# A first modulation in plain float32 on four column quarters, a fixed order of its loads, and sums over partitions that end in a transpose

## Chip, cores and metric

One core of a Trainium2 chip (trn2) runs the whole program once. The metric is the device time of one execution in microseconds; the median of several executions counts.

## What is computed

Two blocks of two layers each, on 256 tokens of width 1024. The change lies almost wholly in the first block. Cut to what matters:

```
xl, xc = x, ctx                                  # 256 tokens each, width 1024
for l in range(2):
    mod  = silu(c)     @ w_mod[l] + b_mod[l]     # 1024 -> 6 * 1024
    modc = silu(c_ctx) @ w_mod[l] + b_mod[l]
    sh1, sc1, gt1, sh2, sc2, gt2 = split(mod, 6) # same for modc
    h = rms_norm(xl, g_pre_mix[l]) * (1 + sc1) + sh1        # and hc from xc
    y, yc = token_mixer(h, hc, ..., w_in[l], ...)
    xl = xl + gt1 * rms_norm(y, g_post_mix[l])
    h = rms_norm(xl, g_pre_ffn[l]) * (1 + sc2) + sh2
    xl = xl + gt2 * rms_norm(swiglu(h, w_ffn_in[l], w_ffn_out[l]), g_post_ffn[l])
    # layer 0 does the same for xc
```

The second block has two more layers with attention and an FFN of the same size; it needs no modulation, but its norms use the same sums.

## The kernel before, in words

Activations lie feature-major: 128 features on the partitions, tokens along the columns (512 columns while both streams run, 256 later). A float32 product is made of three matmuls in the `float32r` type (`mm3`, L164 to L166): high part times high part, high times low, low times high. Weights come in loads of 1 MB (`raw`, L124, two buffers, issued by SP); each is cut into two pieces, and for each piece ACT makes the high part (`whi`, L154) and DVE or POOL the low part (`wlo`, L155). Four pieces (`RING`) can stand ready. A planner (`emit`) calls each piece's `prep` as soon as the ring has room, in the order in which the steps of the program use the pieces. A scheduling layer then puts each engine's instructions in an order of its own; only what is pinned (`pin`) keeps the order of the program.

The program's beginning is what the change touches most. `setup` loads `c`, `c_ctx` (SP) and `x`, `ctx` (ACT) and makes silu(c) as `st1`, 128 columns wide per feature block and zero but for four columns: two streams, each as a high and a low part. `mod(l, g)` (L433 on) makes 512 of the 6144 columns of the modulation. It loads eight tiles of 128 x 512 from `w_mod`, splits every one (ACT L257, DVE L258), and does two matmuls of 512 columns per tile (L447, L448). `mod_flush` copies the 32 rows out on ACT (L502), transposes them on DVE (L503), adds high and low parts in four pieces (L507) and adds the bias (L510). For layer 0 the four groups 2, 3, 0, 1 are done so, 32 tiles in all: these are `sc1` and `sh1`. Between the first two groups stands `x_in`: squares of the input rows on ACT (L1096), 32 transposes on PE (L1106), 1/rms on DVE. Then `pre0` broadcasts 1/rms over the partitions (L316) and makes the eight pairs of high and low parts of `h` (`norm_mod`: DVE L558, ACT L560, DVE L561); the mixer's first matmul with `w_in` needs the first pair.

All other groups of the modulation are made on DVE while PE works at something else (`mod_v`): a loaded half (`mraw`, L458, two buffers) is multiplied by silu(c), one scalar per partition, and added up (L478), and the sum over the 128 partitions is left to PE. `flush` does that with four matmuls per stream that have 128 columns of the sums as the stationary operand and one column of ones as the moving one (L484). The norms take their sums over the features in the same way: `y_rms` after the mixer and the FFN (L611, L612; for three quantities when the residual's norm is made at once), `col_rms` elsewhere (L307).

```
nc.tensor.matmul(ps[:, 4 * i + t:4 * i + t + 1], accs[g][i][:, 128 * t:128 * t + 128],
                 self.ones[:, 0:1], start=True, stop=True)
```

Of the kernel before, what the change touches and what calls it, by code (L numbers as in the profile page):

```python
# [14 lines left out]
D = 1024  # L15
# [30 lines left out]
class Kern:  # L46
# [64 lines left out]
    def pieces(self, loads, na, nb, cuts, perm=False):  # L111
        box = {}
        out = []
        for i, (a0, a1, b0, b1) in enumerate(cuts):
# [3 lines left out]
            def prep(p=p, i=i, a0=a0, a1=a1, b0=b0, b1=b1):  # L118
                nc = self.nc
                if i == 0:  # L120
                    raw = self.static("raw", 2048, RAWS)
                    box["raw"] = raw[:, : na * nb].rearrange("p (a b) -> p a b", a=na)
                    for view, src in loads:
                        nc.sync.dma_start(view(box["raw"]), src)  # L124
                src = box["raw"][:, a0:a1, b0:b1]
# [17 lines left out]
                if perm:  # L143
                    assert a0 == 0 and a1 == na and hb == 128
                    for q in range(2):
                        for h2 in range(2):
                            s_ = src[:, :, 64 * h2:64 * h2 + 64].rearrange(
                                "p a (b q i) -> p a q b i", b=2, q=2, i=16)[:, :, q]
                            o = [x[:, :, 64 * h2:64 * h2 + 64].rearrange(
                                "p a (q b i) -> p a q b i", b=2, q=2, i=16)[:, :, q] for x in (p.hi, p.lo)]  # L150
                            nc.scalar.activation(o[0], s_, AF.Copy)
                            eng.tensor_tensor(o[1], s_, o[0], op=ALU.subtract)
                else:
                    nc.scalar.activation(p.hi, src, AF.Copy)  # L154
                    eng.tensor_tensor(p.lo, src, p.hi, op=ALU.subtract)  # L155

# [11 lines left out]
    def lin(self, st, W, c0, ncols, rhs, N, evac, perm=False, K=8, tok=None, order=None):  # L168
# [5 lines left out]
        for c in range(0, ncols, wide):  # L174
# [4 lines left out]
            for i, p in enumerate(ps_):  # L179
                for j in range(0, cuts[i][3] - cuts[i][2], 128):  # L180
                    def run(t0, t1, p=p, j=j):
                        ps = self.lin_ps()
                        r = rhs()
                        for i, k in enumerate(order or range(K)):
                            rk = [v[:, t0:t1] for v in r[k]]
                            self.mm3(ps[:, t0:t1], (p.hi[:, k, j:j + 128], p.lo[:, k, j:j + 128]), rk,
                                     i == 0, i == K - 1)
                        return ps
# [9 lines left out]
                    st.append(("x", cost, f, (p,), [lambda t=t, run=run, m=m: evac(m, run(*t), t)  # L198
                                                    for t in ((0, N // 2), (N // 2, N))]))

# [100 lines left out]
    def col_rms(self, key, nt, dim):  # L301

        nc = self.nc
        acc = self.v.pop(key)
        ps = self.tr_ps()
        for t in range(nt):
            nc.tensor.matmul(ps[:, t:t + 1], acc[:, 128 * t:128 * t + 128], self.ones[:, 0:1], start=True, stop=True)  # L307
        v = self.small([128, nt])
        nc.vector.tensor_scalar(v, ps[:, :nt], 1.0 / dim, EPS, op0=ALU.mult, op1=ALU.add)
        return self.rsqrt(v, nt)  # L310
# [32 lines left out]
    def setup(self):  # L343
# [8 lines left out]
        nc.vector.memset(self.ones, 1.0)  # L352
        self.twos = self.const([128, 1], "twos")
        nc.vector.memset(self.twos, 2.0)
# [12 lines left out]
        nc.vector.tensor_tensor(cc, cc, th, op=ALU.mult)  # L367
        self.st1 = self.const([128, 8, 128], "st1", F32R)
        nc.vector.memset(self.st1.bitcast(F32), 0.0)
        v = cc.rearrange("p (s k) -> p k s", s=2)  # L370
        nc.vector.tensor_copy(self.st1[:, :, 0:2], v)
        nc.vector.tensor_tensor(self.st1[:, :, 2:4], v, self.st1[:, :, 0:2], op=ALU.subtract)
        self.cc = cc
# [58 lines left out]

    def mod(self, l, g):  # L433

        nc = self.nc
        raw = []
        for k in range(8):
            w = self.slot()
            nc.sync.dma_start(w, self.a["w_mod"][l, 128 * k:128 * k + 128, 512 * g:512 * g + 512])
            raw.append(w)  # L440

        def f():
            ps = self.lin_ps()
            for k in range(8):
# [11 lines left out]
    def mraw(self, l, g, h):  # L456
        w = self.wp.tile([128, 2, 512], F32, name=self.nm("mraw"), tag="mraw", bufs=MRAWS)
        self.nc.sync.dma_start(w, self.a["w_mod"][l, 256 * h:256 * h + 256, 512 * g:512 * g + 512].rearrange(  # L458
            "(k p) c -> p k c", p=128))
        return w  # L460

    def mod_v(self, st, l, groups, streams):
# [17 lines left out]
        def flush(g):  # L480
            ps = self.tr_ps()
            for i in range(streams):
                for t in range(4):
                    nc.tensor.matmul(ps[:, 4 * i + t:4 * i + t + 1], accs[g][i][:, 128 * t:128 * t + 128],  # L484
                                     self.ones[:, 0:1], start=True, stop=True)
            del accs[g]
            b = self.par["b_mod", l][:, 4 * g:4 * g + 4]
            for i in range(streams):
                nc.vector.tensor_tensor(self.mc[l][:, 4 * g:4 * g + 4, i], ps[:, 4 * i:4 * i + 4], b, op=ALU.add)

# [5 lines left out]
        st.append(("x", 0.05, lambda: flush(groups[-1])))  # L496

    def mod_flush(self, l, g, ps):
        nc = self.nc
        rw = self.slot()  # L500
        tw = self.slot()
        nc.scalar.activation(rw[0:32, :], ps[0:32, :], AF.Copy)  # L502
        nc.vector.transpose(tw[0:32, :], rw[0:32, :])  # L503
        v = tw[0:32, :].rearrange("p (t q r) -> p t q r", t=4, q=4)
        mc = self.mc[l]
        for q in range(4):
            nc.vector.tensor_tensor(mc[32 * q:32 * q + 32, 4 * g:4 * g + 4, :], v[:, :, q, 0:2], v[:, :, q, 2:4],  # L507
                                    op=ALU.add)
        b = self.par["b_mod", l][:, 4 * g:4 * g + 4]
        nc.vector.tensor_tensor(mc[:, 4 * g:4 * g + 4, :], mc[:, 4 * g:4 * g + 4, :],  # L510
                                b[:, :, None].to_broadcast([128, 4, 2]), op=ALU.add)

# [57 lines left out]
    def y_add(self, m, ps, tok, full):  # L570
# [26 lines left out]
        if full:  # L597
            put(1, lambda o: nc.vector.tensor_tensor(o[:, c], z[:, c], x[:, c], op=ALU.mult))
            put(2, lambda o: nc.scalar.activation(o[:, c], z[:, c], AF.Square))

    def y_rms(self, t0, full):

        nc, V = self.nc, self.v
        n = 3 if full else 1
        ps = self.tr_ps()
        for i in range(n):
            for t in range(2):
                c = slice(t0 + 128 * t, t0 + 128 * t + 128)
                o = ps[:, 2 * i + t:2 * i + t + 1]
                w = self.ones[:, 0:1] if i != 1 else self.twos  # L610
                nc.tensor.matmul(o, V["acc", i][:, c], w, start=True, stop=False)  # L611
                nc.tensor.matmul(o, V["last", i][:, c], w, start=False, stop=True)  # L612
        v = self.small([128, 2])
        nc.vector.tensor_scalar(v, ps[:, 0:2], 1.0 / D, EPS, op0=ALU.mult, op1=ALU.add)
        if full:
            S = self.small([128, 4])
            nc.vector.tensor_copy(S, ps[:, 2:6])
        r = self.rsqrt(v, 2)
        out = self.bcast(r, 2)
        V["rb"] = out  # L620
        if full:
# [4 lines left out]
            for t in range(2):  # L626
                c = slice(t, t + 1)
                nc.vector.scalar_tensor_tensor(b[:, c], S[:, 2 + t:3 + t], r[:, c], S[:, c], op0=ALU.mult, op1=ALU.add)
            for t in range(2):
# [455 lines left out]
    def block1(self):  # L1085
# [27 lines left out]
        def pre(l, N, t0, s_scale, s_shift, gain):  # L1113
# [4 lines left out]
            return lambda i, rb, t1: self.norm_mod(i, t0, t1, rb, V["A"], self.sec(l, s_shift))  # L1118

        def pre0():  # L1120
            f = pre(0, 512, 0, 1, 0, "g_pre_mix")
            rb = self.bcast(V["r0"], 4)
            for i in range(8):
                f(i, rb, 512)

        def join(l, N, t0, s_scale, s_shift, gain, hot):
# [9 lines left out]
        for l in range(2):  # L1136
            N = 512 if l == 0 else 256
            if l == 0:
                fs = [self.mod(0, g) for g in (2, 3, 0, 1)]
                st.append(X(fs[0]))  # L1140
                st.append(X(x_in))
                st += [X(f) for f in fs[1:]]
                st.append(H(pre0))
# [18 lines left out]
            P_ = lambda p: st.append(X(lambda: setattr(self, "phase", p), 0))  # L1162
            P_(2 * l)
            st += mix
            P_(2 * l + 1)
# [649 lines left out]
def emit(steps, bufs):  # L1815
# [11 lines left out]
    for i, s in enumerate(steps):  # L1827
        if len(s) > 3:
            while nxt < len(order):
                p = order[nxt]  # L1830
                j = p.at - bufs[p.ring]
                if j >= 0 and rings[p.ring][j].end >= i:
                    break
                p.prep()
                nxt += 1
# [85 lines left out]
```

## Time and profile before

| | |
|---|---|
| three runs | 2300.19, 2303.47, 2305.83 us (median 2303.47) |
| the profiled execution | 2300.08 us, span of the profile 2297.9 us |
| PE busy | 2172.5 us, 95% of the span |
| DVE, ACT, POOL busy | 1622.3, 1083.9, 508.1 us |
| mean granted TensorE clock | 0.969 of 2.4 GHz |

The span is read from the first instruction to the last; 2.2 us of the execution lie outside it. A busy PE is not a PE at its peak, since matmuls overlap: their ends are modelled, and a matmul's price is read from one start to the next. A float32 matmul (not `float32r`) stands in the trace as two records. Column counts in the rows are partitions x elements, the stationary operand with a `*`.

### The profile page before, as it was taken

How to read it: one execution, taken by the hardware profiler on the slowest of the kernel's cores; microseconds unless marked ns; L12 is line 12 of the kernel's file. 1: busy time of each engine (PE TensorE's matmuls, PEld its weight loads, DVE VectorE, ACT ScalarE, POOL GpSimd, SP SyncE). 2: the span in 40 equal slices, each digit the busy share in tenths (PEclk: the TensorE clock that was granted, in tenths of full speed). 3: DMA queues.
4: the chain of work that ended last, by engine and by line, in shares of the span. 5: the costliest groups of instructions: out<-in, count | busy, mean ns of one | idle time of the engine just before them, and what ended most of it. 6: DMA issues, size and time to landing. Idle time of an engine off the chain costs nothing.

```text
span 2297.9 us, 37350 instructions
## 1 busy us (share of the span) xinstructions
PE 2172.5 (95%) x14512; PEld 1970.2 (86%) x14512; DVE 1622.3 (71%) x3259; ACT 1083.9 (47%) x2098; POOL 508.1 (22%) x513
## 2 busy tenths in 40 slices
PE   4999999999989999998999899999978999999998
PEld 3777777788888888888888899899976999988998
DVE  5577777858778845567978877765685766676665
ACT  5355565332432222244556555554446544466443
POOL 2354443321230011032333311100243100110000
PEclk8999999999989999998999999999997999999999
DMA  8321112335515656444322455465441555543553
GB/s 277 79 90 56 56 56 74 114 132 180 165 38 159 187 179 199 155 155 128 119 74 86 136 175 178 137 203 183 152 114 53 166 183 181 194 154 105 183 180 120
DMA packets 296626, 319.18 MB, mean 139 GB/s; under 512 B 20545, under 2 KB 264353, under 8 KB 296449
## 3 DMA queue, kind: packets, MB, share of 16 engines
q1 hardware_dynamic: 293072, 311.27, 42.0%
q0 software_dynamic: 2224, 3.43, 0.6%
q8 instruction: 114, 1.87, 0.3%
q10 hardware_dynamic: 1152, 2.10, 0.3%
q14 instruction: 64, 0.52, 0.1%
HBM read 315.72 MB, written 1.05 MB: 138 GB/s over the span
## 4 chain that ended last, share of the span: by engine, by line
PE 71%; DVE 16%; ACT 5%; issue 4%; DMA 2%; POOL 1%; ACTq 0%; DVEq 0%; POOLq 0%; SPq 0%
PE p L164 20%; PE p L165 20%; PE p L166 20%; DVE wlo L155 3%; DVE t L796 1%; PE p L743 1%; DVE t L478 1%; PE p L247 1%; PE p L249 1%; PE tr L883 1%; PE p L248 1%; DVE b L855 1%; PE tr L484 1%; DVE t L258 1%; ACT whi L154 1%
## 5 line engine op out<-in xcount | busy, mean ns | idle before, releaser
L164 PE MATMUL p<-t,whi 128*128 128x256 f32 (+1 forms) x3724 | 1177.1, 320 | 12.6 <-ACT t L560 6.3
L165 PE MATMUL p<-t,whi 128*128 128x256 f32 (+1 forms) x3724 | 1178.3, 317 | 6.3 <-DVE t L659 3.1
L166 PE MATMUL p<-t,wlo 128*128 128x256 f32 (+1 forms) x3724 | 1176.6, 317 | 2.9 <-DVE wlo L155 1.6
L164 PEld LDWEIGHTS p<-t,whi 128*128 128x128 f32 x3724 | 715.8, 194 | 63.8 <-ACT t L560 7.9
L165 PEld LDWEIGHTS p<-t,whi 128*128 128x128 f32 x3724 | 719.8, 193 | 50.4 <-DVE t L659 4.5
L166 PEld LDWEIGHTS p<-t,wlo 128*128 128x128 f32 x3724 | 718.7, 193 | 47.9 <-DVE wlo L155 3.2
L154 ACT ACTIVATE whi<-raw 128x1024 fp32r<-128x1024 f32 (+4 forms) x487 | 491.8, 1020 | 522.9 <-PE p L165 341.5
L155 DVE TENSOR_TENSOR wlo<-raw,whi 128x1024 fp32r<-128x1024 f32 (+4 forms) x443 | 546.1, 1234 | 184.8 <-ACT whi L154 86.5
L155 POOL TENSOR_TENSOR wlo<-raw,whi 128x1024 fp32r<-128x1024 f32 (+2 forms) x44 | 104.2, 2368 | 505.1 <-ACT whi L154 462.7
L478 DVE SCALAR_TENSOR_TENSOR t<-mraw,big,t 128x512 f32<-128x512 f32 x224 | 166.6, 782 | 24.7 <-DMA mraw<-in_w_mod_dram 23.4
L794 POOL TENSOR_TENSOR t<-t,t 128x512 f32<-128x512 f32 (+1 forms) x120 | 137.6, 1147 | 190.0 <-ACT t L793 187.4
L260 ACT ACTIVATE t<-t 128x256 fp32r<-128x256 f32 (+1 forms) x115 | 54.4, 473 | 160.6 <-DVE t L689 118.4
L299 POOL TENSOR_TENSOR t<-t,t 128x256 f32<-128x256 f32 (+1 forms) x27 | 27.1, 1002 | 413.3 <-ACT t L297 412.8
L247 PE MATMUL p<-whi,t 128*128 128x256 f32 x352 | 102.7, 292 | 2.7 <-ACT t L858 2.7
L689 DVE TENSOR_TENSOR t<-t,p 128x256 f32<-128x256 f32 (+1 forms) x91 | 43.2, 474 | 84.0 <-PE p L166 83.9
L796 DVE SCALAR_TENSOR_TENSOR t<-u,big,t 128x512 f32<-128x512 f32 (+1 forms) x120 | 100.7, 839 | 0.8
L743 PE MATMUL p<-t,t 64*128 64x256 f32 (+2 forms) x528 | 77.7, 378 | 23.8 <-DVE t L261 11.7
L249 PE MATMUL p<-whi,t 128*128 128x256 f32 x352 | 100.0, 284 | 0.0
L248 PE MATMUL p<-wlo,t 128*128 128x256 f32 x352 | 99.9, 284 | 0.0
L594 POOL TENSOR_TENSOR t<-t,t 128x256 f32<-128x256 f32 (+1 forms) x36 | 40.5, 1153 | 220.6 <-ACT t L596 217.3
L743 PEld LDWEIGHTS p<-t,t 64*128 64x128 f32 x528 | 50.8, 212 | 44.8 <-issue 18.1
L257 ACT ACTIVATE t<-p 128x256 fp32r<-128x256 f32 x72 | 27.6, 383 | 122.1 <-DVE p L726 98.9
(298 smaller groups left out, 2542.6 us busy)
## 6 DMA issues: line engine op xcount, KB each, us to landing
raw<-in_w_in_dram SPq DMA_DIRECT2D x60, 1024.0 KB, 5.1
raw<-in_l_w_gate_up_dram SPq DMA_DIRECT2D x44, 1024.0 KB, 5.1
raw<-in_w_ffn_in_dram SPq DMA_DIRECT2D x42, 1024.0 KB, 5.2
mraw<-in_w_mod_dram SPq DMA_DIRECT2D x80, 512.0 KB, 4.4
raw<-in_l_w_in_dram SPq DMA_DIRECT2D x15, 1024.0 KB, 5.1
raw<-in_l_w_down_dram SPq DMA_DIRECT2D x16, 896.0 KB, 5.0
t<-in_w_mod_dram SPq DMA_DIRECT2D x32, 256.0 KB, 5.3
raw<-in_w_attn_out_dram SPq DMA_DIRECT2D x8, 1024.0 KB, 5.3
```

Of the source, the lines that this page charges most:

```text
L154: nc.scalar.activation(p.hi, src, AF.Copy)
L155: eng.tensor_tensor(p.lo, src, p.hi, op=ALU.subtract)
L164: mm(ps, lh, rh, start=first, stop=False)
L165: mm(ps, lh, rl, start=False, stop=False)
L166: mm(ps, ll, rh, start=False, stop=last)
L247: mm(ps[:, :256], lh, p.hi[:, k % 4], start=k == 0, stop=False)
L248: mm(ps[:, :256], lh, p.lo[:, k % 4], start=False, stop=False)
L249: mm(ps[:, :256], ll, p.hi[:, k % 4], start=False, stop=k == 7)
L478: nc.vector.scalar_tensor_tensor(acc, w[:, k], c, acc, op0=ALU.mult, op1=ALU.add)
L743: self.nc.tensor.matmul(out[half], q[i // 2][h, qs], k[i % 2][h, ks], start=i == 0, stop=i == 2)
L794: nc.gpsimd.tensor_tensor(acc, acc, t, op=ALU.add)
L796: i = nc.vector.scalar_tensor_tensor(acc, u, w, acc, op0=ALU.mult, op1=ALU.add)
```

## The change

`mod(l)` now does all four groups, 0 to 3, in one step. `st1` is a plain float32 tile of 32 columns per feature block, two of them not zero. A loaded tile is not split: it goes to PE as it is, in four matmuls of 128 columns, one per quarter `q`, whose results lie on partitions 32q to 32q+31. The columns are picked so that a DVE transpose of 32 x 32 blocks brings each of them to its partition. The order of the steps becomes `x_in`, `mod`, first pieces, `pre0`.

`flush`, `y_rms` and `col_rms` get the same form: now the ones (32 columns) are stationary, the sums move, in four column quarters, and a DVE transpose puts the totals on the partitions (`col_sums`).

The loads of the first two `raw` tiles and the splits of their pieces are pinned to the program's order, as are all `mraw` loads; the first two pieces are prepared ahead of `pre0`, the next two in its middle, and the first two steps of the mixer run as one (`together`), a feature block at a time.

```diff
-                        nc.sync.dma_start(view(box["raw"]), src)
+                        i_ = nc.sync.dma_start(view(box["raw"]), src)
+                        if self.rings["raw"][1] <= RAWS:
+                            self.pin(i_)
...
+    def together(self, steps):
+
+        def f():
+            gs = [s[5]() for s in steps]
+            for ps in zip(*gs):
+                pass
+            for s, x in zip(steps, ps):
+                s[6](x)
+        return ("x", sum(s[1] for s in steps), f, tuple(p for s in steps for p in s[3]))
...
-        ps = self.tr_ps()
-        for t in range(nt):
-            nc.tensor.matmul(ps[:, t:t + 1], acc[:, 128 * t:128 * t + 128], self.ones[:, 0:1], start=True, stop=True)
+        S = self.col_sums([[acc[:, :128 * nt]]], nt)
...
-        self.st1 = self.const([128, 8, 128], "st1", F32R)
+        self.st1 = self.cp.tile([128, 8, 32], F32, name="st1")
...
         def f():
-            ps = self.lin_ps()
-            for k in range(8):
-                hi, lo = self.slot(F32R), self.slot(F32R)
-                self.split(hi, lo, raw[k])
-                nc.tensor.matmul(ps, self.st1[:, k], hi, start=k == 0, stop=False)
-                nc.tensor.matmul(ps, self.st1[:, k], lo, start=False, stop=k == 7)
-            self.mod_flush(l, g, ps)
+            t = self.slot()
+            for g in range(4):
+                ps = self.lin_ps()
+                for k in range(8):
+                    w = raw[g, k].rearrange("p (t q r) -> p q t r", q=4, r=32)
+                    for q in range(4):
+                        nc.tensor.matmul(ps[32 * q:32 * q + 32, :128], self.st1[:, k], w[:, q],
+                                         start=k == 0, stop=k == 7)
+                c = slice(128 * g, 128 * g + 128)
+                nc.vector.transpose(t[:, c], ps[:, :128])
+                m = slice(4 * g, 4 * g + 4)
+                nc.vector.tensor_tensor(self.mc[l][:, m, :], t[:, c].rearrange("p (m c) -> p m c", c=32)[:, :, 0:2],
+                                        self.par["b_mod", l][:, m, None].to_broadcast([128, 4, 2]), op=ALU.add)
...
-        self.nc.sync.dma_start(w, self.a["w_mod"][l, 256 * h:256 * h + 256, 512 * g:512 * g + 512].rearrange(
-            "(k p) c -> p k c", p=128))
+        self.pin(self.nc.sync.dma_start(w, self.a["w_mod"][l, 256 * h:256 * h + 256, 512 * g:512 * g + 512].rearrange(
+            "(k p) c -> p k c", p=128)))
...
             for i in range(streams):
-                for t in range(4):
-                    nc.tensor.matmul(ps[:, 4 * i + t:4 * i + t + 1], accs[g][i][:, 128 * t:128 * t + 128],
-                                     self.ones[:, 0:1], start=True, stop=True)
+                a = accs[g][i].rearrange("p (t q r) -> p q t r", q=4, r=32)
+                for q in range(4):
+                    nc.tensor.matmul(ps[32 * q:32 * q + 32, 128 * i:128 * i + 128], self.ones[:, 0:32], a[:, q],
+                                     start=True, stop=True)
...
+        n = 128 * streams
+        t = self.slot()[:, :n]
+        nc.vector.transpose(t, ps[:, :n])
...
+    def col_sums(self, terms, nt):
...
+        for i, xs in enumerate(terms):
+            w = self.twos if i == 1 else self.ones[:, 0:32]
+            for j, x in enumerate(xs):
+                v = x.rearrange("p (t q r) -> p q t r", q=4, r=32)
+                for q in range(4):
+                    nc.tensor.matmul(ps[32 * q:32 * q + 32, m * i:m * i + m], w, v[:, q],
+                                     start=j == 0, stop=j == len(xs) - 1)
+        n = m * len(terms)
+        t = self.slot()[:, :n]
+        nc.vector.transpose(t, ps[:, :n])
...
-                fs = [self.mod(0, g) for g in (2, 3, 0, 1)]
-                st.append(X(fs[0]))
+                f = self.mod(0)
                 st.append(X(x_in))
-                st += [X(f) for f in fs[1:]]
+                st.append(X(f))
+                at0 = len(st)
                 st.append(H(pre0))
...
+                early += [s[3][0] for s in mix[2:4]]
+                first = [s[3][0] for s in mix[:2]]
+                st.insert(at0, X(lambda first=first: [p.prep() for p in first]))
+                mix = [self.together(mix[:2])] + mix[2:]
```

The order in which SP issues its first loads, before the change (`raw` is a 1 MB weight load, `t` here a 256 KB tile of `w_mod`):

```order
L350 DMA big<-in_k_ident_dram 128x128
L124 DMA raw<-in_w_in_dram 128x8x256 x2
L439 DMA t_117<-in_w_mod_dram 128x512
...
L439 DMA t_179<-in_w_mod_dram 128x512
L124 DMA raw<-in_w_in_dram 128x8x256 x2
L458 DMA mraw_3928<-in_w_mod_dram 128x2x512
L458 DMA mraw_3968<-in_w_mod_dram 128x2x512
L124 DMA raw<-in_w_in_dram 128x8x256 x18
```

And with the change:

```order
L369 DMA big<-in_k_ident_dram 128x128
L458 DMA t_116<-in_w_mod_dram 128x512
...
L458 DMA t_178<-in_w_mod_dram 128x512
L124 DMA raw<-in_w_in_dram 128x8x256 x22
L124 DMA raw<-in_w_conv_out_dram 128x4x512 x2
L124 DMA raw<-in_w_in_dram 128x8x256 x2
L482 DMA mraw_3838<-in_w_mod_dram 128x2x512
```

The two weight loads that stood ahead of the 32 tiles of `w_mod` now stand behind them, and the first `mraw` loads have moved from the beginning to behind 26 weight loads.

DVE around the last group of the modulation and the first of `h`, before:

```order
L258 TENSOR_TENSOR t_483<-t_177,t_482 128x512
L258 TENSOR_TENSOR t_489<-t_179,t_488 128x512
L503 STREAM_TRANSPOSE t_495<-t_494 32x512
L558 SCALAR_TENSOR_TENSOR t_526<-t_278,c_503,tr_521 128x256 x2
L507 TENSOR_TENSOR big<-t_495 32x8 x3
L561 SCALAR_TENSOR_TENSOR t_506<-t_526,big,t_505 128x256
```

And with the change (`wlo_414` and `wlo_418` are the low parts of the first two pieces, of the first weight load):

```order
L470 STREAM_TRANSPOSE t_270<-p_376 128x128
L472 TENSOR_TENSOR big<-t_270,big 128x8
L157 TENSOR_TENSOR wlo_414<-raw,whi_413 128x1024
L535 SCALAR_TENSOR_TENSOR c_421<-big 128x16
L157 TENSOR_TENSOR wlo_418<-raw,whi_417 128x1024
L573 SCALAR_TENSOR_TENSOR t_444<-t_219,c_421,tr_439 128x256 x2
L576 SCALAR_TENSOR_TENSOR t_424<-t_444,big,t_423 128x256
```

The low parts of the first weight load, which DVE did at the start before, now stand right ahead of `norm_mod`.

PE at the first flush of `mod_v` with two streams, before:

```order
L166 MATMUL p_4168<-t_519,wlo_4050 128x512
L484 MATMUL tr_4195<-big,t_3930 128x1 x4
L484 MATMUL tr_4195<-big,t_3931 128x1 x4
L164 MATMUL p_4219<-t_3742,whi_4089 128x512
L165 MATMUL p_4219<-t_3743,whi_4089 128x512
```

And with the change:

```order
L171 MATMUL p_4078<-t_437,wlo_3960 128x512
L510 MATMUL tr_4105<-t_3840,big 32x128 x4
L510 MATMUL tr_4105<-t_3841,big 32x128 x4
L169 MATMUL p_4130<-t_3652,whi_3999 128x512
L170 MATMUL p_4130<-t_3653,whi_3999 128x512
```

The flush keeps its place among the mixer's matmuls; its matmuls have 32 stationary columns and 128 moving ones instead of 128 and one.

## Rows read from the trace of the kernel before

**Rows 1.** The page: busy time and share of the span.
```profile
PE 2172.5 (95%) x14512; PEld 1970.2 (86%) x14512; DVE 1622.3 (71%) x3259; ACT 1083.9 (47%) x2098; POOL 508.1 (22%) x513
```
**Rows 2.** Busy time by stretch: length, PE, PEld, DVE, ACT, POOL, clock, DMA, GB/s.
```profile
30.00:40.00 10.00, 5.25 (x24) 4.33 (x23) 4.59 (x19) 10.00 (x26) 0.00 (x0) 0.68 1.07 377
50.00:60.00 10.00, 7.93 (x20) 5.42 (x19) 6.27 (x15) 4.75 (x9) 5.52 (x11) 0.67 0.03 7
...
400.00:640.00 240.00, 237.55 (x1186) 201.34 (x1185) 181.91 (x274) 82.61 (x123) 60.17 (x37) 0.98 0.44 142
685.00:1035.00 350.00, 349.99 (x1766) 299.07 (x1767) 232.02 (x340) 103.31 (x155) 51.12 (x26) 1.00 0.53 170
```
**Rows 3.** Timeline of ACT at the beginning: start, length, what, [idle before <-releaser].
```profile
2.66 5.18 ACTq L361 DMA_DIRECT2D t<-in_ctx_dram  x4
12.11 2.00 ACT L154 ACTIVATE whi<-raw 128x1024 fp32r<-128x1024 f32 x2 [2.73 <-DMA raw<-in_w_in_dram]
51.94 4.25 ACT L257 ACTIVATE t<-t 128x512 fp32r<-128x512 f32 x8
```
**Rows 4.** Timeline of DVE at the beginning.
```profile
13.20 2.36 DVE L155 TENSOR_TENSOR wlo<-raw,whi 128x1024 fp32r<-128x1024 f32 x2 [2.98 <-ACT whi L154]
54.66 3.69 DVE L258 TENSOR_TENSOR t<-t,t 128x512 fp32r<-128x512 f32 x6
61.92 0.82 DVE L558 SCALAR_TENSOR_TENSOR t<-t,c,tr 128x256 f32<-128x256 f32 x2
```
**Rows 5.** Timeline of PE at the beginning.
```profile
27.53 3.65 PE L1106 MATMUL p<-big,t 128*128 128x128 f32 x32
35.93 2.05 PE L316 MATMUL tr<-big,c 128*128 128x128 f32 x8 [4.75 <-DVE c L284]
63.34 1.25 PE L164 MATMUL p<-t,whi 128*128 128x512 f32 x4 [2.71 <-ACT t L560]
```
**Rows 6.** SP's issues at the beginning; then loads and the median us to landing.
```profile
1.92 2.05 SPq L124 DMA_DIRECT2D raw<-in_w_in_dram  x2
12.11 20.66 SPq L439 DMA_DIRECT2D t<-in_w_mod_dram  x32
t<-in_w_mod_dram SPq DMA_DIRECT2D x32, 256.0 KB, 5.3
t<-in_ctx_dram ACTq DMA_DIRECT2D x4, 256.0 KB, 7.1
```
**Rows 7.** PE in column halves (64 stationary columns): the beginning of one call, the end of another.
```profile
1736.74 0.28 PE L164 MATMUL p<-t,whi 128*128 128x256 f32 x1
1736.94 1.28 PE L1261 MATMUL tr<-t,t 128*64 128x256 f32 x8
...
2082.59 0.61 PE L1261 MATMUL tr<-t,t 128*64 128x128 f32 x8
```
**Rows 8.** PE at a flush with two streams and one with one; then the line in all.
```profile
535.83 1.84 PE L484 MATMUL tr<-big,t 128*128 128x1 f32 x16
537.53 0.49 PE L164 MATMUL p<-t,whi 128*128 128x512 f32 x1
...
873.23 0.95 PE L484 MATMUL tr<-big,t 128*128 128x1 f32 x8
874.03 0.49 PE L164 MATMUL p<-t,whi 128*128 128x512 f32 x1
L484 PE MATMUL tr<-big,t 128*128 128x1 f32 x256 | 29.8, 244 | 0.7 <-DVE t L478 0.7
```
**Rows 9.** PE, the sums of the norms, by line: busy us, mean ns | idle before.
```profile
L611 PE MATMUL tr<-big,t 128*128 128x1 f32 x64 | 11.9, 255 | 3.1 <-DVE t L594 3.1
L612 PE MATMUL tr<-big,t 128*128 128x1 f32 x64 | 11.4, 248 | 0.0
L307 PE MATMUL tr<-big,t 128*128 128x1 f32 x32 | 4.4, 246 | 3.2 <-DVE t L299 3.2
```
**Rows 10.** Who waited for the `mraw` loads, whole span: us, times.
```profile
  DVE t L478: 23.4, 17
```

More of the change, by code (lines that the diff above doesn't have):

```diff
@@ L153, in prep @@
                 else:
-                    nc.scalar.activation(p.hi, src, AF.Copy)
-                    eng.tensor_tensor(p.lo, src, p.hi, op=ALU.subtract)
+                    i1 = nc.scalar.activation(p.hi, src, AF.Copy)
+                    i2 = eng.tensor_tensor(p.lo, src, p.hi, op=ALU.subtract)
+                    if self.rings["raw"][1] <= RAWS:
+                        self.pin(i1)
+                        self.pin(i2)
             p.prep = prep
@@ L180, in lin, with gen @@
                 for j in range(0, cuts[i][3] - cuts[i][2], 128):
-                    def run(t0, t1, p=p, j=j):
+                    def gen(t0, t1, p=p, j=j):
                         ps = self.lin_ps()
@@ L187, in run @@
                                      i == 0, i == K - 1)
+                            yield ps
+                    def run(t0, t1, gen=gen):
+                        for ps in gen(t0, t1):
+                            pass
                         return ps
@@ L198, in lin @@
                     st.append(("x", cost, f, (p,), [lambda t=t, run=run, m=m: evac(m, run(*t), t)
-                                                    for t in ((0, N // 2), (N // 2, N))]))
+                                                    for t in ((0, N // 2), (N // 2, N))],
+                               lambda gen=gen: gen(0, N), lambda ps, m=m: evac(m, ps)))
+    def together(self, steps):
+        def f():
+            gs = [s[5]() for s in steps]
+            for ps in zip(*gs):
+                pass
+            for s, x in zip(steps, ps):
+                s[6](x)
+        return ("x", sum(s[1] for s in steps), f, tuple(p for s in steps for p in s[3]))
     def lin_pair(self, st, Wa, ca, Wb, cb, n, rhs, N, evac_a, evac_b):
@@ L430, in setup_rest, with mod @@
             self.par[name] = cols[:, 8 * i:8 * i + 8]
-    def mod(self, l, g):
+    def mod(self, l):
         nc = self.nc
-        raw = []
-        for k in range(8):
-            w = self.slot()
-            nc.sync.dma_start(w, self.a["w_mod"][l, 128 * k:128 * k + 128, 512 * g:512 * g + 512])
-            raw.append(w)
-        def f():
-            ps = self.lin_ps()
-            for k in range(8):
-                hi, lo = self.slot(F32R), self.slot(F32R)
-                self.split(hi, lo, raw[k])
-                nc.tensor.matmul(ps, self.st1[:, k], hi, start=k == 0, stop=False)
-                nc.tensor.matmul(ps, self.st1[:, k], lo, start=False, stop=k == 7)
-            self.mod_flush(l, g, ps)
+        raw = {}
+        for g in range(4):
+            for k in range(8):
+                w = raw[g, k] = self.slot()
+                nc.sync.dma_start(w, self.a["w_mod"][l, 128 * k:128 * k + 128, 512 * g:512 * g + 512])
+        def f():
+            t = self.slot()
+            for g in range(4):
+                ps = self.lin_ps()
+                for k in range(8):
+                    w = raw[g, k].rearrange("p (t q r) -> p q t r", q=4, r=32)
[7 more added lines that the diff above has]
+                                        self.par["b_mod", l][:, m, None].to_broadcast([128, 4, 2]), op=ALU.add)
         return f
@@ L496, in mod_v @@
         st.append(("x", 0.05, lambda: flush(groups[-1])))
[L498 to L511, printed above, removed]
     def sec(self, l, s):
@@ L599, in y_add @@
             put(2, lambda o: nc.scalar.activation(o[:, c], z[:, c], AF.Square))
+    def col_sums(self, terms, nt):
+        nc = self.nc
+        ps = self.tr_ps()
+        m = 32 * nt
+        for i, xs in enumerate(terms):
[8 more added lines that the diff above has]
+        nc.vector.transpose(t, ps[:, :n])
+        return t.rearrange("p (i t c) -> p i t c", t=nt, c=32)[:, :, :, 0]
     def y_rms(self, t0, full):
@@ L604, in y_rms @@
         n = 3 if full else 1
[L605 to L612, printed above, removed]
+        S = self.col_sums([[V[x, i][:, t0:t0 + 256] for x in ("acc", "last")] for i in range(n)], 2)
         v = self.small([128, 2])
[L614 to L617, printed above, removed]
+        nc.vector.tensor_scalar(v, S[:, 0], 1.0 / D, EPS, op0=ALU.mult, op1=ALU.add)
         r = self.rsqrt(v, 2)
@@ L1118, in pre @@
             return lambda i, rb, t1: self.norm_mod(i, t0, t1, rb, V["A"], self.sec(l, s_shift))
+        early = []
         def pre0():
@@ L1124, in pre0 @@
                 f(i, rb, 512)
+                if i == 3:
+                    for p in early:
+                        p.prep()
         def join(l, N, t0, s_scale, s_shift, gain, hot):
@@ L1833, in emit @@
                     break
-                p.prep()
+                if p.hi is None:
+                    p.prep()
                 nxt += 1
```

20 lines of the change are left out of this document (10 added, 10 removed).

## The prediction

> **What bounds the kernel now.** I read the page first. PE is busy 95% of the span and DVE 71% [rows 1], so time is gained by doing less on PE, or by ending a stretch in which PE waits. The table of stretches tells the two apart [rows 2]: from 400 to 640 us and from 685 to 1035 us PE is busy 99 to 100% of the time and DVE 66 to 76%. There PE time that goes away shortens the run one to one, up to the point where DVE is the last. The beginning is the other kind. The first matmul of the mixer starts only at 63.34 us [rows 5]; from 50 to 60 us the DMA engines move 7 GB/s against 377 from 30 to 40 us, so the loads are over by then. What is left is splitting: eight tiles cost ACT 4.25 us, .53 each, and six cost DVE 3.69 us, .61 each [rows 3, 4].
>
> The sum is made against the profiled execution, 2300.08 us, which lies .15% under the median of the three runs, 2303.47 us. 0.3% of it is 6.9 us, about what a measurement can tell from no change.
>
> **The price of a matmul in quarters.** A float32 pass over 128 columns: 32 transposes start within 3.65 us less the .27 of the last one, over 31 gaps .109 us [rows 5]; that was at full clock. A float32 matmul is two passes. If four quarters run beside each other, four matmuls of 128 columns cost 2 x .109 = .22 us; in pairs .44; one after another .87. Four at once are nowhere in the trace, but halves are: eight records of 128 columns with 64 stationary columns take .61 us [rows 7], less .27 for the last .34, over seven gaps .049 each, half of .109. So two halves do run beside each other; I take four for quarters and keep the pairs and the series as bounds. Entering this form costs little: the matmul of 256 columns before the halves holds PE .20 us (1736.74 to 1736.94), where its columns alone are worth about .11 to .12; I take .08 at entry and as much at the exit, .17 in all.
>
> The Trainium skill, TensorE: Matmul & The Clock Gate, Back-to-back issue gap, says that in a real stream of weight loads and matmuls of 128 columns each takes about 81 ns. By that as a floor per record a flush of two streams would cost 16 x .081 + .17 = 1.47 us (an estimate from that page) the gain at the flushes would shrink to some 3 us, and the whole would be about 2277, inside the range; the halves at 49 ns [rows 7] don't agree with a floor so high, so I don't take it.
>
> **1. The beginning.** Two raw loads of 1 MB go from ahead of the 32 tiles to behind them. SP issues the last tile at 12.11 + 20.66 = 32.77 less its own .33, and it lands 5.3 us later [rows 6], at 37.7. Without 2.1 MB ahead at 377 GB/s [rows 2], 5.6 us, that is 32.1. Can PE keep up? Its inputs: `ctx` is issued until 7.84 [rows 3] and lands 7.1 us later [rows 6], at 15; transposes 3.65, some gaps, and PE is free for the tiles from about 20 us. A tile is .22 us at full clock, and .43 at the clock of .67 to .68 that the beginning is granted, where the 1.2 GHz level shows half the time [rows 2]: 7 to 14 us for 32 tiles, done when the last one lands. The splits of the tiles are gone from ACT and DVE.
>
> Then the first raw load is last. It lands 1 MB after the tiles, 2.8 to 3.0 us: 35.1. ACT's high part takes 1.0 us [rows 3], DVE's low parts 1.18 each [rows 4], and in the order of DVE both stand ahead of the first norm; with .2 for the columns in between, 38.7. From the first norm instruction to the first mixer matmul it took 61.92 to 63.34 [rows 4, 5], 1.42 us. **First mixer matmul at 40.1 us, 23.2 earlier.** Behind it not all is kept: two steps run as one, six matmuls per feature block (1.3 us), but DVE gives a block in four instructions of .4 [rows 4], and the low part of the third piece, 1.18, stands in between. I take off 1.7 us: **-21.5** (bounds -18 and -25). The broadcast of 1/rms (2.05 us [rows 5]) lies under the loads. What POOL loads and splits in this stretch has its time until the mixer's fourth piece, and is costed at nothing; if that cover is thin, the lower bound has it.
>
> **2. The flushes.** 256 records [rows 8] are 128 matmuls, 32 streams: twelve flushes with two, eight with one. With two, PE is held from 535.83 to 537.53, 1.70 us; with one .80. Now 4 passes of .109 and the switch of .17: .61; with one stream .39. 12 x 1.09 + 8 x .41 = **-16.4** (in pairs -9.5; in series +4.4). These lie in stretches where PE is always busy [rows 2], so I count all of it. The rule against that stands in the Trainium skill, TensorE: Matmul & The Clock Gate, Measured speedup vs the span model: three column tiles gave 2.38, not 3. By it (an estimate from that page) 4 passes are worth .55 instead of .44, and this term would be about 14.6; the halves at .049 instead of .054 [rows 7] show no such loss, so I stay with the row.
>
> DVE gets a transpose of 128 x 256 and an addition per flush, some .4 us each, where DVE is idle a quarter of the time: nothing. The `mraw` loads are pinned behind the weight loads on SP. DVE waited for them 23.4 us in 17 places already [rows 10], and PE ended no stall with that; nothing, unless they come much later, which is a rival.
>
> **3. The norms.** The lines L611 and L612 have 64 records each, five full sums of 24 and a rest of 8, at some .10 us [rows 9]: 2.45 us for one full sum, PE otherwise idle, since the next work needs the norm. In quarters it is about 6 passes, .65, the switch, and a transpose of 128 x 192 on DVE of about .35 behind it: 1.0. 5 x 1.45 = **-7** (bounds -3 and -9). `col_rms`, 32 records and 4.4 us in all [rows 9], gains as much as its transposes cost: nothing.
>
> Sum: 21.5 + 16.4 + 7 = 45, so 2255 us for an execution like the profiled one. Since that one is 3.4 us under the median, I say **2257**.
>
> **Rivals.**
> (a) *Only two quarters at a time*, that is, the halves' .05 us per record is the floor. For it: nothing faster is in the trace. Against it: the halves' gap is exactly half a pass, so it is the columns that bound them. Flushes -9.5, norms -4; a tile costs .44 to .87, the mod ends at 34 to 48 us, the front gives about -16.5. Sum -30: **2270**. Chance .14.
> (b) *The freed PE time turns into waits.* DVE at 66 to 76% with new transposes, the `mraw` loads in a fixed order [rows 10]: PE would then stand at each flush as long as it was busy before. The front alone, -21.5: **2279**. Against it: only DVE waits there today. Chance .15.
> (c) *The other side: quarters run one after another.* The place is the 32 tiles at the beginning. 256 passes at the clock of .67 [rows 2], some .16 us each, are 41 us from 20.2 on; the first mixer matmul comes at 65.7, +2.4, the flushes give +4.4 and the norms +2.5: **2309**, slower. It decides from about .124 us a pass on, where the front's gain is the 6.9 us that flushes and norms lose. The halves [rows 7] speak against it. Chance .07.
> The main case has what is left, .64, and by its bounds lies between 2246 and 2266.
>
> **How the numbers follow.** The range takes the main case from its lower end, then (a) and (b) up to 2281, and leaves out (c) and the tails: 2246 to 2281. Slower by over 0.3% is (c), less what of it ends within 0.3%, .05; no change takes .02 of it and as much of a front that fails together with (b), .04; faster .91.
>
> **What the profile would show.** Right: the last `w_mod` tile lands near 32 us, the first mixer matmul starts near 40 instead of 63.34; four records of a pass start together, a tile every .22 or .43 us; two-stream flushes of .6 us and one-stream of .4; norm sums of .8 us with a transpose behind them; and PE still busy 99% from 400 to 1000 us. Wrong: records of quarters .05 us or .11 us apart throughout (a, c); stalls of PE released by DVE or by `mraw` near the flushes (b); or the first matmul held by something other than DVE's low parts, such as POOL's loads or the second raw tile.

## The result, and the profile after

The changed kernel takes 2279.64 us, median of 4 runs (2278.46 to 2281.37), against 2301.83 before: 22.2 us less, a ratio of .9905 (95% interval .9887 to .9924). Forecast were 45 us less, 2257, with a range of 2246 to 2281. The sign was right, the size was off by half; the time lies inside the range, but where rival (b) stands and not the main case. The page's busy line, then two of the stretches of [rows 2] and a third one, with the columns shown there:

```profile
PE 2139.7 (94%) x14856; PEld 1925.2 (84%) x14856; DVE 1627.5 (71%) x3226; ACT 1064.8 (47%) x2060; POOL 509.6 (22%) x513
```
```profile
400.00:640.00 240.00, 231.92 (x1296) 195.73 (x1295) 190.29 (x293) 83.79 (x134) 64.25 (x46) 0.98 0.45 144
685.00:1035.00 350.00, 341.19 (x1776) 282.94 (x1775) 240.16 (x377) 110.56 (x163) 62.87 (x35) 0.99 0.54 172
1100.00:1500.00 400.00, 373.02 (x2910) 355.35 (x2909) 308.79 (x629) 225.45 (x445) 86.41 (x112) 0.97 0.41 134
```

The third stretch in the kernel before:

```profile
1100.00:1500.00 400.00, 379.59 (x2893) 358.47 (x2892) 318.35 (x654) 230.79 (x459) 99.52 (x127) 0.99 0.41 134
```

PE is busy 33 us less than before [rows 1], but the span shrank by 18 only: PE now also stands where it hardly stood before, 8.1 us from 400 to 640 and 8.8 from 685 to 1035, and from 1100 to 1500 it stands 27.0 us instead of 20.4.

To see where the time went, compare when each kernel starts the n-th matmul of the split products (L164 to L166 before, L169 to L171 after; 11,532 in both). This count is worked out from the two traces:

```
n-th matmul      before, us   change is ahead by, us
1                     63.34        20.0
1001                 438.5         21.4
4001                1089.0         37.1
5601                1414.6         33.1
6001                1477.9         25.9
7201                1623.7         27.7
7601                1706.9         19.3
last                2287.2         18.3
```

At 1089 us the change is 37 us ahead, where the terms of the forecast have some 44 by there (21.5, 16.4 and four norms). Against a second profile of the kernel before (e11 below) it is only 30. Then 7 us are lost between 1415 and 1478, 8 between 1624 and 1707. The steps themselves, 8.0 and 7.7 us, are the same against either profile. Nothing of the change stands there but sums of norms. DVE at the first place:

```profile
1399.49 1.23 DVE L157 TENSOR_TENSOR wlo<-raw,whi 128x1024 fp32r<-128x1024 f32 x1 [2.58 <-ACT whi L156]
1400.63 0.42 DVE L279 TENSOR_TENSOR t<-p,t 128x256 fp32r<-128x256 f32 x1
1402.36 1.23 DVE L157 TENSOR_TENSOR wlo<-raw,whi 128x1024 fp32r<-128x1024 f32 x1 [1.31 <-ACT whi L156]
1403.50 0.42 DVE L279 TENSOR_TENSOR t<-p,t 128x256 fp32r<-128x256 f32 x1
1406.80 1.23 DVE L157 TENSOR_TENSOR wlo<-raw,whi 128x1024 fp32r<-128x1024 f32 x1 [2.88 <-ACT whi L156]
1407.94 0.38 DVE L631 STREAM_TRANSPOSE t<-tr 128x192 f32<-128x192 f32 x1
```

And PE, the last sums, the broadcast of 1/rms that waits for them, and the next product:

```profile
1397.15 0.37 PE L627 MATMUL tr<-t,big 128*32 128x64 f32 x11
...
1411.43 1.22 PE L335 MATMUL tr<-big,c 128*128 128x128 f32 x4 [4.32 <-DVE c L300]
1415.51 1.22 PE L335 MATMUL tr<-big,c 128*128 128x128 f32 x4 [2.86 <-DVE c L300]
1419.83 0.58 PE L169 MATMUL p<-t,whi 128*128 128x256 f32 x1 [3.10 <-ACT t L575]
```

The last sums end near 1397.7. Their transpose (L631) takes .38 us, as reckoned, but starts 10.3 us later. It stands in DVE's queue behind three low parts, each of which waits for its high part, and behind two splits whose inputs PE makes only after the sums. DVE idles 6.8 us in the three waits of these rows. PE then stands three times, 10.3 us in all. The other place is alike:

```profile
1621.94 1.23 DVE L157 TENSOR_TENSOR wlo<-raw,whi 128x1024 fp32r<-128x1024 f32 x1 [2.23 <-ACT whi L156]
1624.29 1.23 DVE L157 TENSOR_TENSOR wlo<-raw,whi 128x1024 fp32r<-128x1024 f32 x1 [1.12 <-ACT whi L156]
1625.43 0.24 DVE L631 STREAM_TRANSPOSE t<-tr 128x64 f32<-128x64 f32 x1
```
```profile
1629.91 1.20 PE L335 MATMUL tr<-big,c 128*128 128x128 f32 x4 [5.31 <-DVE c L300]
1633.80 0.58 PE L169 MATMUL p<-t,whi 128*128 128x256 f32 x1 [2.70 <-ACT t L681]
```

In the kernel before, the DVE instruction that took the sums out of PSUM at the same step of the program started at once:

```profile
1432.04 0.16 DVE L614 TENSOR_SCALAR c<-tr 128x2 f32<-128x2 f32 x1 [3.35 <-PE tr L612]
```

The beginning of the changed kernel, SP, ACT, DVE and PE, answers to [rows 3 to 6]:

```profile
4.21 26.05 SPq L458 DMA_DIRECT2D t<-in_w_mod_dram  x32
t<-in_w_mod_dram SPq DMA_DIRECT2D x32, 256.0 KB, 5.4
```
```profile
38.40 2.00 ACT L156 ACTIVATE whi<-raw 128x1024 fp32r<-128x1024 f32 x2 [17.35 <-DMA raw<-in_w_in_dram]
39.48 1.23 DVE L157 TENSOR_TENSOR wlo<-raw,whi 128x1024 fp32r<-128x1024 f32 x1 [2.84 <-ACT whi L156]
41.85 0.87 DVE L573 SCALAR_TENSOR_TENSOR t<-t,c,tr 128x256 f32<-128x256 f32 x2
```
```profile
20.34 6.19 PE L467 MATMUL p<-t,st 128*32 128x128 f32 x152
...
43.36 1.22 PE L169 MATMUL p<-t,whi 128*128 128x512 f32 x2 [7.30 <-ACT t L575]
```

And the flushes, one with two streams and one with one, to [rows 8]:

```profile
514.27 0.65 PE L510 MATMUL tr<-t,big 128*32 128x128 f32 x16
514.84 0.50 PE L169 MATMUL p<-t,whi 128*128 128x512 f32 x1
...
863.46 0.43 PE L510 MATMUL tr<-t,big 128*32 128x128 f32 x8
863.81 0.50 PE L169 MATMUL p<-t,whi 128*128 128x512 f32 x1
```

From the first row to the second .57 us, where .61 was forecast; from the third to the fourth .35, forecast .39. In the trace's single records the first four start within .02 us of each other (514.269 to 514.289), the next four .13 us later, the others every .11. So the four quarters do run beside each other. The matmul just ahead of these sums holds PE .32 us, where it held .23 ahead of the old ones; with that, a flush of two streams saves 1.04 us, not 1.09.

### The profile page after: what moved, and what is told of

Its sections match the earlier page's. It is cut to its first block, busy times and chain, and to the rows that moved or that the text cites. A ratio compares the mean times of both kernels' runs of the same rounds, so it can differ in the third digit from the quotient of the medians.

```text
span 2279.6 us, 37970 instructions
## 1 busy us (share of the span) xinstructions
PE 2139.7 (94%) x14856; PEld 1925.2 (84%) x14856; DVE 1627.5 (71%) x3226; ACT 1064.8 (47%) x2060; POOL 509.6 (22%) x513
## 5 line engine op out<-in xcount | busy, mean ns | idle before, releaser
L169 PE MATMUL p<-t,whi 128*128 128x256 f32 (+1 forms) x3724 | 1175.5, 319 | 23.3 <-ACT t L575 11.1
L171 PE MATMUL p<-t,wlo 128*128 128x256 f32 (+1 forms) x3724 | 1173.0, 316 | 1.2 <-POOL wlo L157 1.1
L156 ACT ACTIVATE whi<-raw 128x1024 fp32r<-128x1024 f32 (+4 forms) x487 | 497.7, 1024 | 769.1 <-PE p L170 625.2
L169 PEld LDWEIGHTS p<-t,whi 128*128 128x128 f32 x3724 | 713.5, 193 | 78.6 <-ACT t L575 12.2
L171 PEld LDWEIGHTS p<-t,wlo 128*128 128x128 f32 x3724 | 717.4, 193 | 44.6 <-POOL wlo L157 1.3
L502 DVE SCALAR_TENSOR_TENSOR t<-mraw,big,t 128x512 f32<-128x512 f32 x224 | 172.3, 806 | 23.5 <-DMA mraw<-in_w_mod_dram 22.2
L320 POOL TENSOR_TENSOR t<-t,t 128x256 f32<-128x256 f32 (+1 forms) x27 | 28.8, 1065 | 411.0 <-ACT t L318 367.8
L609 POOL TENSOR_TENSOR t<-t,t 128x256 f32<-128x256 f32 (+1 forms) x36 | 43.6, 1240 | 220.4 <-ACT t L611 220.3
```

The costliest lines, as they stand in the source:

```text
L156: i1 = nc.scalar.activation(p.hi, src, AF.Copy)
L169: mm(ps, lh, rh, start=first, stop=False)
L171: mm(ps, ll, rh, start=False, stop=last)
L502: nc.vector.scalar_tensor_tensor(acc, w[:, k], c, acc, op0=ALU.mult, op1=ALU.add)
```

## Experiments

Theory A of most runs: the transpose of a norm writes a slot of the ring of 66 tiles that nearly all activations share; slots go out in the program's order, so the scheduling layer cannot move the transpose ahead of work that is written earlier and takes slots too. Before, the sums were read into small tiles with buffers of their own. Rival: PE time that is taken away turns into waits for DVE whatever the order.

**e1, a tile of its own for the norms' transposes.**

```diff
-        t = self.slot()[:, :n]
+        t = self.sp.tile([128, 192], F32, name=self.nm("s"), tag="sums", bufs=2)[:, :n]
```

> The changed kernel, but the transpose that ends a norm's sum writes a tile of its own pool (two buffers of 192 columns) instead of the next slot of the ring of 66 that all other activations share. Theory A (the ring hands its slots out in the program's order, so the transpose stands on DVE behind low parts and mem_kv's splits that are written ahead of it, and the two stalls of 10.3 and 11.0 us behind the sums at 1397.7 and 1614.5 us come from there): the transposes at these two places start within 1 us of the sums' end, PE's waits there shrink by 16 to 19 us, and the kernel takes 2261 to 2264 us. Theory B (PE time that goes away turns into waits for DVE and the loads whatever the order): 2277 to 2281 us, and the waits move elsewhere.

2266.6 us (2265.08 to 2268.13), ratio .9846 (.9826 to .9865): 13.0 less than the change, a little less than expected. DVE and PE at the first place:

```profile
1391.85 0.38 DVE L631 STREAM_TRANSPOSE s<-tr 128x192 f32<-128x192 f32 x1 [0.85 <-PE tr L627]
```
```profile
1391.24 0.54 PE L627 MATMUL tr<-t,big 128*32 128x64 f32 x24
1401.15 0.71 PE L335 MATMUL tr<-big,c 128*128 128x128 f32 x4 [0.40 <-DVE c L300]
```

The transpose now starts with the end of the sums, and PE waits .40 us at the broadcast; all its waits around this place come to 3.1 us, where the change has 10.3 and the kernel before 3.4. It is ahead of before by 39 us at the 5601st matmul and 37.6 at the 7201st; nothing is lost at the two places. One line of code, and nothing else of the arithmetic, gives the 13 us back.

**e10, two more slots**, `SLOTS` 68 instead of 66.

> The changed kernel with 68 slots in the shared ring instead of 66. Theory A (what holds the transposes is the order in which slots are handed out, not that too few are free): the two transposes start 10 to 11 us behind the sums as before, 2277 to 2282 us. Theory B (too few free slots): they start earlier, 2266 to 2272.

2280.28 us, one run; what decides here is its trace. The transpose at the first place still stands behind the same low parts, 10.3 us after the sums:

```profile
1405.39 1.22 DVE L157 TENSOR_TENSOR wlo<-raw,whi 128x1024 fp32r<-128x1024 f32 x1 [2.88 <-ACT whi L156]
1406.53 0.38 DVE L631 STREAM_TRANSPOSE t<-tr 128x192 f32<-128x192 f32 x1
```

So it is not two missing slots. That it is the order of handing out fits both runs, but is argued and not shown; how the scheduling layer decides was not looked into further.

**e2, e3, e4: each part alone.** e2 is the change with the flush and the norms of before; e3 and e4 are the kernel before with one of the two loops.

```diff
-                nc.tensor.matmul(o, V["acc", i][:, c], w, start=True, stop=False)
-                nc.tensor.matmul(o, V["last", i][:, c], w, start=False, stop=True)
+        S = self.col_sums([[V[x, i][:, t0:t0 + 256] for x in ("acc", "last")] for i in range(n)], 2)
```

> The new beginning (modulation in quarters, order of the loads, pins, two steps together) with the flushes and the norms of the kernel before. Theory A: the beginning keeps what it gained at the first mixer matmul, 20 us, less 1 to 2, so 18 to 19 us less than before, 2283 to 2285. Theory B: its gain is lost again on the way; within 5 us of before, 2297 to 2302.

> The kernel before with only the flushes in quarters. Theory A: a flush with two streams .60 us instead of 1.70, and with one .4 instead of .8; 12 to 16 us less, 2286 to 2290. Theory B: PE waits in their place, within 4 us of before, 2298 to 2302.

> The kernel before with only the sums of the norms in quarters and a transpose into a slot of the shared ring. Theory A: 4 to 8 us gained at the norms, 18 to 20 us lost at the two transposes that stand late on DVE; 10 to 16 us slower than before, 2312 to 2318. Theory B: no place loses 10 us; 2294 to 2302.

e2 2286.33, e3 2290.53, e4 2299.23 us, against 2301.71: 15.4, 11.2 and 2.5 less. The 2.5 of e4 can't be told from no change (ratio .9992, .9980 to 1.0004). For e4 theory A had the place and not the sum: by the count of matmuls it is 18.3 ahead at the 4001st, 11.4 against the second profile of the kernel before, then loses 7.9 at each of the two late transposes (against either profile), which stand in the same order on DVE as in the change. For e2 and e3 theory A comes nearer, but both gave less than it said.

**e5, the flushes' transposes in a tile of their own too.**

```diff
-            t = self.slot()[:, :n]
+            t = self.sp.tile([128, 256], F32, name=self.nm("s"), tag="fl", bufs=1)[:, :n]
```

> As e1_own_tile, and the transposes of the flushes also write a tile of their own (one buffer of 256 columns), so that none of the change's transposes takes a slot of the shared ring. In the changed kernel the flush's transpose starts up to 8.5 us after its matmuls. Theory A (these delays lie beside PE's work, since the modulation is needed only later): the same as e1_own_tile, 2264 to 2268 us. Theory B (they cost PE waits, as at 572 and 1000 us, where PE waits 3.5 and 4.7 us for DVE's sums): 3 to 5 us less, 2261 to 2264.

2267.65 us (2265.59 to 2272.12), as e1. Late transposes of the flushes cost nothing: nobody is waiting for them.

**e6 and e7: two parts together**, the beginning with the norms of e1 (old flushes), and the beginning with the flushes (old norms).

> The new beginning and the new norms with their own tile, and the flushes of the kernel before. Theory A (a norm in quarters is worth about 3 us, half of it because TensorE's clock no longer falls to 1.2 GHz behind the one-column sums, as it does in the kernel before from 634.4 to 637.7 us): e2_only_front less 14 to 17 us, 2269 to 2273. Theory B (only the sums' own time counts, 1.45 us for five norms): e2_only_front less 6 to 8 us, 2278 to 2281.

> The new beginning and the new flushes with the norms of the kernel before. Theory A (the late transposes of the norms took back what the norms gained): e2_only_front less what e3_only_flush gained, 10 to 12 us, so 2274 to 2277, a little faster than the whole change. Theory B (beginning and flushes hinder each other): above 2280.

e6 2277.22, e7 2279.29 us, against 2301.35. e6 lies nearer to theory B: on top of e2 the norms give 9 us, not 14 to 17. e7 falls between its two. The whole change equals e7 to .4 us: **the norms, as the change makes them, are worth nothing**; with their own tile (e1) they are worth 13 on top of e7. The flushes are worth 7 on top of e2 and 11 on top of e6 (differences from before: e2 15.4, e7 22.1, e6 24.1, e1 35.1). Added in the order beginning, norms with their own tile, flushes, shared slot, the steps are 15.4, 8.7, 11.0 and -13.0, where 21.5, 7, 16.4 and nothing were forecast. So -6.1, +1.7, -5.4 and -13.0 make up the 22.8 us that are missing; in another order the parts would be shared out differently.

**e8, no pin on the first two weight loads.**

```diff
-                        if self.rings["raw"][1] <= RAWS:
-                            self.pin(i_)
```

> The changed kernel without the pin on the first two weight loads; they go ahead of the 32 tiles again, and the low parts keep their place behind the modulation on DVE. Theory A (the beginning is bound by the bytes that must land and the chain behind them): the last tile lands at 37.5 to 38.4 us instead of 35.4, the two low parts (2.4 us) and the norm (1.9) follow it, and the first mixer matmul starts at 43 to 44 us, as with the pin (43.4). Theory B (the order of the loads is what gained): 46 us or later.

2283.65 us, one run, against 2279.64 for the change. The first product lies between the two theories, at 45.45 us, since the last tile lands later than I thought, at 40.4. By one profile of each, the order of the loads is worth 2 us at the first product.

**e9, the norm's first block ahead of the first low parts**, on top of e1.

```diff
-                st.insert(at0, X(lambda first=first: [p.prep() for p in first]))
...
+                if i == 0:
+                    for p in early[:2]:
+                        p.prep()
```

> As e1_own_tile, and the first two pieces are prepared behind the first block of the first norm instead of ahead of it, so that on DVE the low parts no longer stand between the modulation and the norm. In the changed kernel the first weight load lands at 38.4 us, the low parts end at 41.9, and only then the norm begins. Theory A (the first mixer matmul waits for the chain low parts, then norm): it starts at 39.5 to 40.5 us instead of 43.4, and the kernel is 2 to 4 us faster than e1_own_tile, 2262 to 2265. Theory B (the blocks of the norm, 1.6 us each on DVE, set the pace behind it anyway): an earlier start, but at most 1 us is left of it at the 200th mixer matmul; 2265 to 2268.

2266.86 us, as e1: theory B. The first product starts at 40.45 us instead of 43.4 in the change, but by the 201st only 1.1 us is left against e1. DVE's blocks set the pace, not the start: from 37.9 to 56.6 us DVE idles .6 us in e9.

**e11, e12: two kernels profiled again.**

> The kernel before, unchanged, profiled once more: how much of the 6 us that the beginning's gain loses behind 1100 us (20.5 us at 1082 us, 13.3 at the end in the profile of e2_only_front) lies in the one profile of the kernel before. Theory A (the profile of before has a quick second half by chance): from the 4001st mixer matmul to the end it takes 3 to 6 us longer than the 1201.2 us of the first profile. Theory B (the beginning's change costs it there): within 1.5 us of 1201.2.

> e2_only_front unchanged, profiled once more. Theory A: from the 4001st mixer matmul to the end it differs from the 1208.4 us of its first profile by 2 us or more. Theory B: within 1.5 us of 1208.4.

Theory B in both. From the 4001st product to the last, the kernel before takes 1198.2 and 1198.3 us in its two profiles, the new beginning alone 1205.3 and 1204.3 (the numbers in the expectations start some twenty matmuls earlier). So the 6 to 7 us that the beginning loses there come again. At places in between, the two profiles of before still lie up to 4 us apart. The whole profile of e11 was 6.8 us shorter than the first one, nearly all of it between 390 and 650 us. There the first profile has the clock at 1.2 GHz from 392.0 to 395.4, 409.1 to 412.5 and 600.2 to 603.6, where e11 has it at 2.4, and once 3.4 us longer, from 644.6 on; each time it falls 1.2 to 2.0 us behind. A single profile is no measure to 3 us; the medians are a better one.

## Why the forecast was half wrong

By the steps of the prediction:

- **The price of quarters: right.** .57 and .35 us where .61 and .39 stood, or .66 and .44 with the .09 us by which the matmul ahead is held. Rivals (a) and (c) fall by these rows.
- **The beginning: right in its chain, 3 us off in the loads, and 6 to 7 lost later.** From the landed weights (38.4) to the first product (43.36) it took 5.0 us, as forecast. But the first tile is issued at 4.21 us and the last lands at about 35.3 (4.21 + 26.05 - .33 + 5.4), not at 32.1, and so the first weight load lands at 38.4 instead of 35.1. From 8 to 24 us the DMA engines now move 318 GB/s, where they moved 374 before; that is .9 MB less, or some 2.4 us of loading at 377 GB/s (an estimate). What holds them back isn't shown. How much of the 5.6 us came back is open too: the last tile lands at 37.8 in the first profile of the kernel before and at 39.9 in e11. At 111 us the change is 18.2 ahead (I said 21.5). In e2 the lead falls from 20.5 to 13.3 behind 1089 us in steps of 1 to 2.3 us, where no line of the beginning runs; e11 and e12 show that it repeats. Two of the steps are waits of PE that the kernel before has hardly or not at all: 1.35 us for ACT at 1986.9 us (.27 and .13 in the two profiles of before) and 1.04 for DVE at 2049.5 (none); e12 has the same two, 1.35 and 1.10. Why the orders differ there stays open. By the medians, 15.4 of the 21.5 us are left.
- **The flushes: the price right, the cover wrong.** -16.4 was forecast, 7 to 11 came. Ten of the twelve with two streams move the next matmul ahead by 1.0 us each. But I counted all of it because PE was always busy there, and DVE was not far behind. At the last flush of a group PE now stands

```profile
575.63 0.43 PE L510 MATMUL tr<-t,big 128*32 128x128 f32 x8 [3.53 <-DVE t L502]
```

  where it waited .7 before [rows 8]; DVE's sums run back to back there. Ahead of the third norm's sums PE waits longer for DVE, too, 4.65 us where the longest wait before was 3.1 [rows 9]:

```profile
1005.15 0.44 PE L627 MATMUL tr<-t,big 128*32 128x64 f32 x8 [4.65 <-DVE t L609]
```

  That is rival (b), at two places and not at all flushes.
- **The norms: the step that failed.** "A transpose of 128 x 192 on DVE of about .35 behind it: 1.0." The duration was right (.38), and behind the four full sums of the first layer the transpose does start within .4 us. But I priced an instruction and not its place: DVE takes its queue in order (6.0 of the 6.8 us that it idles in the waits above lie behind the end of the sums), and at two norms the transpose stands 10 us back. Part 1 gave the beginning's order on DVE in full; for the norms I read no order at all, though that of the changed kernel has three low parts ahead of the transpose. e1 puts a price on it: 13.0 us, the largest piece of the 22.8 us that are missing. "PE otherwise idle" doesn't hold either: behind the first norm's sums the kernel before runs products until the broadcast, from 634.3 to 637.9 us. The sum of the term held in spite of that, 8.7 us in e6 where 7 were forecast.
- **Rival (b)** named 2279 us, and 2279.6 it was, but for another reason: in it the waits stood at each flush, by DVE's load and the `mraw` order. The waits for `mraw` went from 23.4 us [rows 10] to

```profile
DVE t L502 <- DMA mraw<-in_w_mod_dram: 22.2, 16, 4.6
```

  and more than half of the loss lies at two norms in the second layer, in a queue with idle time in it. That the number came out is luck.
- **Two slips that change nothing above.** Means of .67 and .68 put the low clock at two thirds of those stretches [rows 2], not at half. And the times of the rivals are reckoned from 2300.08 us, the forecast from 1.7 us more.

## What to carry to other kernels

An instruction added to a chain costs its place in its queue, not its length: before giving it a price, read the rows ahead of it in the new order and ask what each of them waits for. A tile taken from a large shared ring may tie an urgent instruction to the program's order; small results on a critical chain get buffers of their own, as in e1 (2266.6 us; e5 and e9, which keep that tile, lie within 1.1 us of it, and no kernel here is faster). And PE at 99% says nothing of how far DVE is behind it: PE time taken out counts only up to the next place where PE must wait for DVE's result.

## What the runs showed of the hardware

**The clock behind one-column sums.** The granted clock in the kernel before, ahead of the first norm's sums, during them, behind them, behind that:

```profile
629.00:631.40 2.40, 2.40 (x21) 2.40 (x21) 0.48 (x3) 0.57 (x2) 0.00 (x0) 1.00 0.00 0
631.60:634.30 2.70, 2.70 (x25) 2.67 (x24) 0.16 (x1) 0.28 (x1) 0.00 (x0) 1.00 0.00 0
634.40:637.70 3.30, 3.30 (x17) 3.30 (x17) 2.54 (x21) 0.00 (x0) 0.00 (x0) 0.50 0.02 5
637.70:640.00 2.30, 2.30 (x21) 2.30 (x21) 1.51 (x3) 2.00 (x4) 1.15 (x1) 0.98 0.00 0
```

and in the changed kernel ahead of the same sums, with them, and behind them:

```profile
603.00:605.00 2.00, 2.00 (x19) 2.00 (x18) 0.94 (x3) 1.05 (x3) 0.00 (x0) 1.00 0.00 0
605.20:608.80 3.60, 3.58 (x69) 3.17 (x68) 1.02 (x3) 1.05 (x3) 0.00 (x0) 1.00 0.02 5
608.80:612.00 3.20, 3.19 (x29) 2.99 (x26) 2.90 (x21) 1.02 (x2) 0.00 (x0) 1.00 0.00 0
```

PE is called busy throughout, and yet the clock falls from 2.4 to 1.2 GHz for 3.3 us, right behind 2.7 us of sums with one moving column. Matmuls of 256 columns then start every .21 us instead of .12; fifteen of them cost 1.4 us, as much as the shorter sums saved, and I had not priced it. Counted over all 14 profiles, 14 to 18 matmuls of the eight microseconds behind the first norm's sums start .18 to .26 us after the one before them in each of the six with one-column sums (before, e2, e3, e7, e11, e12), and 3 in each of the eight with quarters.

It is no rule. Behind the same sums of the second norm the clock of the kernel before stays up:

```profile
669.70:672.60 2.90, 2.90 (x28) 2.90 (x28) 0.05 (x1) 0.51 (x1) 1.10 (x1) 1.00 0.23 79
672.60:679.00 6.40, 5.89 (x48) 5.58 (x48) 6.28 (x41) 0.00 (x0) 0.86 (x1) 1.00 0.01 3
```

In e3 and e12 it falls there, too; what decides isn't shown. Nor is it shown what the fall costs in the whole program: theory A of e6 gave each norm half of its 3 us for it, and the five norms brought 8.7 us instead of 14 to 17. The Trainium skill, TensorE: Matmul & The Clock Gate, What's actually happening, says that half rate is the default and activity releases it. The rows don't speak against that; they show a fall to half rate right behind a stretch in which the page has PE busy without a gap.
